# Layer 2's values and gates as seven half products, and weights split by two loads

## The chip, the cores and the metric

The kernel runs on one core of a Trainium2 chip. The metric is the device time of one execution in microseconds (us). Five engines work side by side, each through a queue of its own in order: TensorE (PE, products into PSUM; PEld is its load of the stationary operand), VectorE (DVE), ScalarE (ACT), GpSimd (POOL) and SyncE (SP, which here only issues DMAs). They wait for each other by semaphores. PSUM has eight banks of 128 x 512 f32.

## The reference

A trunk of two layers over 512 tokens of 2048 features, each layer normalizes its input, mixes, and adds to it. Layer 1 is a convolution branch and an attention branch; the change leaves it alone but for the end. Layer 2, which it touches, is a gated linear recurrence of 16 heads with a state of 128 x 128:

```python
h = rmsnorm(x, od_norm_g[j])
p = h @ od_w_in[j]                       # 2048 -> 4 x 2048
q, f_raw, i_val, g = _split(p, [HGRN_FDIM, HGRN_FDIM, D_MODEL, D_MODEL])
o = hgrn2(q, f_raw, i_val, lb_all[l], hgrn_norm_g[j]) * jax.nn.silu(g)
x = x + o @ od_w_out[j]
```

`i_val` are the values, `g` the gates. All is float32, and the output is normalized once more.

## The kernel before

**Precision.** TensorE works in float32r. Each operand is kept as two parts that add up to it: a rounded copy (ScalarE, `split_plain` or `split_scaled`) and the rest (VectorE). `mm3` makes three matmuls of one product: high by high, high by low, low by high.

**Weights.** They come in the order of use as 288 tiles of 512 KB, each two quarters [128, 512]. `prefetch` loads a tile on SP's queue into one of three buffers, `prepare` splits a quarter into one of four pairs `wh`, `wl`, two quarters ahead of use. A quarter feeds 12 matmuls (`quarter`).

**Chains.** Small dependent work (norms, attention, convolution, recurrence) is written as generators. `tick()` after each quarter moves every chain a step on, so that its instructions stand between dense matmuls; `finish` runs chains to their end with nothing between. TensorE's order is the order of the program; the other engines' is made by a scheduler.

**End of layer 1.** The output projection adds to `xa` (x, one [128, 512] tile per 128 features). In its last 16 columns `to_h1` makes the split, scaled `h1[c]` (names `hh`, `hl`) and sums squares into `acc1`. The factor 1/rms of layer 2 is made in a chain (`rstd_chain`) and applied to results: `rb1` along tokens as columns, `r1` for tokens as rows.

**Layer 2.** For each group of four heads, `value_rows` makes the values of four heads with tokens as rows: `h1` stationary, weights moving, 16 quarters of 12 matmuls into four banks. Then `head(h)` makes three dense products of four quarters each: query, decay (after which the recurrence `hgrn` of the head starts as a chain of 14 steps) and gate. From group 1 on, the projection of the four heads before (`w_out("ow", ...)`, 16 quarters) comes between values and heads. The steps of `hgrn` that the prediction speaks of: two radix stages (L680, with VectorE's L651 to L686), turning the keys (L741, L743), state sums (L747 to L751), output (L757, L759), its norm (squares L762, L764, power L765 on GpSimd, scaling L769), turning back and the gate (L773, L775).

Of the kernel before, what the change touches and what calls it, by code (L numbers as in the profile page):

```python
# [7 lines left out]
F32 = mybir.dt.float32  # L8
# [7 lines left out]
P = 128  # L16
# [12 lines left out]
N_WTILES = 288  # L29
LAST = 2 * N_WTILES - NK  # L30

# columns of the packed per-feature vectors
# [15 lines left out]
def trunk(ctx: ExitStack, tc: tile.TileContext, x, w, vec, cst, rope, msk, out, order):  # L48
# [6 lines left out]
    rawp = ctx.enter_context(tc.tile_pool(name="rawp", bufs=3))  # L55
    wsp = ctx.enter_context(tc.tile_pool(name="wsp", bufs=4))
# [18 lines left out]
    # chains of dependent steps, advanced by one step after each quarter of weights  # L75
# [19 lines left out]
    # the activation table and the tensor engine's clock come up while the first loads are under way  # L95
# [10 lines left out]
    # weights: a stream of quarters [128, 512], split into two float32r parts that add up exactly  # L106
    raws = []
    count = [0, 0]

    def prefetch(parts=1):  # L110
        raw = rawp.tile([P, 2 * S], F32, name="raw", tag="raw")
# [10 lines left out]
    def prepare():  # L122
# [5 lines left out]
        if n >= LAST:  # L128
            t = htile(n - LAST)
        else:  # L130
            t = (wsp.tile([P, S], F32R, name="wh", tag="wh"), wsp.tile([P, S], F32R, name="wl", tag="wl"))
        split_plain(src, *t)
        ready.append(t)

    def next_quarter(key):
# [3 lines left out]
        while len(ready) <= min(n + (AHEAD if n >= 16 else 0), 2 * N_WTILES - 1):  # L139
            prepare()  # L140
        return ready[n]
# [24 lines left out]
    def split_scaled(src, g, hi, lo):  # L166
        """hi + lo = src * g"""
# [47 lines left out]
    def silu2(src, rb, dst):  # L215
        """dst = 2 silu(src * rb)"""
# [7 lines left out]
    # ---------------------------------------------------------------- layer 0  # L224
# [55 lines left out]
    # lb = sigmoid(l1 - l0); la = (1 - lb) / 2  # L280
# [17 lines left out]
    # keep where query (partition) - key (free) >= 0  # L298
# [38 lines left out]
    # the high part on the lower half of the partitions, the low part on the upper one  # L337
# [167 lines left out]
    for g in range(2):  # L505
        # rotary part of the queries: x1 and x2 of four heads, 32 partitions each
# [17 lines left out]
        for j in range(4):  # L524
# [7 lines left out]
            # both parts of the rotary queries, each on both halves of the partitions  # L532
# [10 lines left out]
            # convolution groups spread over the heads  # L543
# [5 lines left out]
    # under the last head  # L549
# [4 lines left out]
    xp = ctx.enter_context(tc.tile_pool(name="xp", bufs=1, side="right", reuse_waits="tile"))  # L554
    xall = xp.tile([P, NK, S], F32, name="xall")
    xa = [xall[:, k, :] for k in range(NK)]

    def load_xa():
        for k in range(NK):
            nc.sync.dma_start(xa[k], x[:, k, :])  # L560
# [3 lines left out]
    spawn(load_xa())  # L564
# [6 lines left out]
    def w_out(name, rows, cols, after=None):  # L571
        n = len(rows)
        ops = [mix[r] for r in rows]
# [8 lines left out]

    acc1 = cp.tile([P, S], F32, name="acc", tag="acc")
    rb1 = cp.tile([P, S], F32, name="rb1", tag="rb")
    r1 = cp.tile([P, 4], F32, name="r1", tag="r0")
    h1 = []
    with ectx as cctx:
# [30 lines left out]
        def to_h1(c):  # L618
            h = htile(c)
            split_scaled(xa[c], vs[:, V_ODG + c:V_ODG + c + 1], *h)  # L620
            add_square(xa[c], acc1, c, pool)
            h1.append(h)

# [3 lines left out]
    # ---------------------------------------------------------------- layer 1  # L627
# [3 lines left out]
    c1 = spawn(rstd_chain(acc1, D, r1, rb1, 2))  # L631
# [331 lines left out]
```

## Time and profile before

| | us |
|---|---|
| median of three runs | 1790.07 (1789.45 to 1792.38) |
| span of the profiled execution, first to last instruction | 1787.5 |
| TensorE busy | 1768.7 (99%) |
| VectorE, ScalarE, GpSimd busy | 1150.6, 673.6, 83.1 |

The profiled execution's time is given as its span; what lies around the span is read from the difference to the runs, 2.6 us to the median. Busy TensorE means that some matmul is in it: matmuls overlap, so how fast it goes is read from their starts. An engine's idle time costs only where TensorE waits for it.

### The profile page before, as it was taken

How to read it: one execution, taken by the hardware profiler on the slowest of the kernel's cores; microseconds unless marked ns; L12 is line 12 of the kernel's file. 1: busy time of each engine (PE TensorE's matmuls, PEld its weight loads, DVE VectorE, ACT ScalarE, POOL GpSimd, SP SyncE). 2: the span in 40 equal slices, each digit the busy share in tenths (PEclk: the TensorE clock that was granted, in tenths of full speed). 3: DMA queues.
4: the chain of work that ended last, by engine and by line, in shares of the span. 5: the costliest groups of instructions: out<-in, count | busy, mean ns of one | idle time of the engine just before them, and what ended most of it. 6: DMA issues, size and time to landing. Idle time of an engine off the chain costs nothing.

```text
span 1787.5 us, 22387 instructions
## 1 busy us (share of the span) xinstructions
PE 1768.7 (99%) x8419; PEld 1470.5 (82%) x8419; DVE 1150.6 (64%) x2313; ACT 673.6 (38%) x1385; POOL 83.1 (5%) x86
## 2 busy tenths in 40 slices
PE   8999999999999999999999999999999999999997
PEld 6888888888888888888888888888888888888887
DVE  8554958595799775652677445776346774567766
ACT  6334444444443223452333222333323332333354
POOL 6000000000000000130000000000000000000000
PEclk9999999999999999999999999999999999999998
DMA  6222222222362232222222222222222222222232
GB/s 233 92 94 89 84 91 82 97 88 94 131 201 101 94 102 93 95 94 95 86 80 83 83 94 86 92 83 77 89 94 88 78 83 83 87 90 83 76 101 95
DMA packets 53612, 172.68 MB, mean 97 GB/s; under 512 B 5632, under 2 KB 9984, under 8 KB 53120
## 3 DMA queue, kind: packets, MB, share of 16 engines
q1 hardware_dynamic: 52928, 170.28, 28.2%
q8 instruction: 66, 1.08, 0.3%
q10 hardware_dynamic: 576, 0.97, 0.2%
q14 instruction: 42, 0.34, 0.1%
HBM read 163.89 MB, written 7.34 MB: 96 GB/s over the span
## 4 chain that ended last, share of the span: by engine, by line
PE 95%; DVE 2%; issue 2%; DMA 1%; ACT 0%; POOL 0%; POOLq 0%; DVEq 0%; ACTq 0%
PE mm L145 28%; PE mm L147 28%; PE mm L146 28%; PE aux L680 2%; PE aux L378 1%; PE aux L727 1%; PE aux L757 1%; DVE wl L173 1%; PE aux L759 1%; PE aux L747 1%; DVE hl L169 1%; DMA raw<-w 1%; PE aux L373 0%; PE aux L773 0%; PE aux L145 0%
## 5 line engine op out<-in xcount | busy, mean ns | idle before, releaser
L172 ACT ACTIVATE wh<-raw 128x512 fp32r<-128x512 f32 x560 | 352.2, 631 | 870.5 <-PE mm L146 737.6
L173 DVE TENSOR_TENSOR wl<-raw,wh 128x512 fp32r<-128x512 f32 x560 | 390.5, 699 | 356.8 <-ACT wh L172 342.2
L145 PE MATMUL mm<-hh,wh 128*128 128x512 f32 x1424 | 569.5, 400 | 1.4 <-ACT wh L172 1.4
L147 PE MATMUL mm<-hh,wl 128*128 128x512 f32 x1424 | 556.0, 390 | 3.0 <-DVE wl L173 3.0
L146 PE MATMUL mm<-hl,wh 128*128 128x512 f32 x1424 | 555.0, 390 | 0.7 <-DVE hl L169 0.7
L147 PEld LDWEIGHTS mm<-hh,wl 128*128 128x128 f32 x1424 | 267.3, 188 | 61.2 <-DVE wl L173 4.2
L145 PEld LDWEIGHTS mm<-hh,wh 128*128 128x128 f32 x1424 | 267.9, 188 | 54.5 <-ACT wh L172 2.3
L146 PEld LDWEIGHTS mm<-hl,wh 128*128 128x128 f32 x1424 | 267.8, 188 | 54.3 <-DVE hl L169 1.5
L427 DVE SCALAR_TENSOR_TENSOR y<-u,cwh,y 128x512 f32<-128x512 f32 x240 | 178.0, 745 | 2.5
L145 PE MATMUL mm<-mh,wh 128*128 128x512 f32 x448 | 178.1, 397 | 0.0
L147 PE MATMUL mm<-mh,wl 128*128 128x512 f32 x448 | 177.1, 395 | 0.0
L146 PE MATMUL mm<-ml,wh 128*128 128x512 f32 x448 | 177.0, 395 | 0.0
L579 DVE TENSOR_TENSOR xall<-xall,mm 128x512 f32<-128x512 f32 x96 | 65.8, 686 | 90.3 <-PE mm L147 90.3
L145 PE MATMUL mm<-wh,hh 128*128 128x512 f32 x256 | 102.1, 399 | 0.0
L147 PEld LDWEIGHTS mm<-mh,wl 128*128 128x128 f32 x448 | 84.2, 188 | 20.2
L146 PEld LDWEIGHTS mm<-ml,wh 128*128 128x128 f32 x448 | 84.2, 188 | 20.0
L145 PEld LDWEIGHTS mm<-mh,wh 128*128 128x128 f32 x448 | 84.2, 188 | 19.7
L147 PE MATMUL mm<-wh,hl 128*128 128x512 f32 x256 | 99.8, 390 | 0.0
L146 PE MATMUL mm<-wl,hh 128*128 128x512 f32 x256 | 99.7, 389 | 0.0
L147 PEld LDWEIGHTS mm<-wh,hl 128*128 128x128 f32 x256 | 48.0, 188 | 10.3
L146 PEld LDWEIGHTS mm<-wl,hh 128*128 128x128 f32 x256 | 48.1, 188 | 9.3
L145 PEld LDWEIGHTS mm<-wh,hh 128*128 128x128 f32 x256 | 48.1, 188 | 9.2
(229 smaller groups left out, 1906.1 us busy)
## 6 DMA issues: line engine op xcount, KB each, us to landing
raw<-w SPq DMA_DIRECT2D x287, 512.0 KB, 3.2
xall<-xT SPq DMA_DIRECT2D x16, 256.0 KB, 5.0
x<-xT SPq DMA_DIRECT2D x3, 1024.0 KB, 7.6
mix<-m SPq DMA_DIRECT2D x12, 256.0 KB, 2.0
m<-mix SPq DMA_DIRECT2D x12, 256.0 KB, 2.8
out<-xall SPq DMA_DIRECT2D x6, 512.0 KB, 3.1
x<-xT SPq DMA_DIRECT2D x4, 256.0 KB, 4.9
out<-xall SPq DMA_DIRECT2D x4, 256.0 KB, 3.5
```

The source lines that it names most:

```text
L145: pe.matmul(ps, a[0][:, asl], b[0][:, bsl], start=first, stop=False)
L146: pe.matmul(ps, a[0][:, asl], b[1][:, bsl], start=False, stop=False)
L147: pe.matmul(ps, a[1][:, asl], b[0][:, bsl], start=False, stop=last)
L169: dve.scalar_tensor_tensor(out=lo, in0=src, scalar=g, in1=hi.bitcast(F32), op0=ALU.mult, op1=ALU.subtract)
L172: act.activation(hi, src, AF.Copy)
L173: dve.tensor_tensor(out=lo, in0=src, in1=hi.bitcast(F32), op=ALU.subtract)
L378: pe.matmul(po[:, jb * P:], vr[:, jb, blocks(j)], pts[jb], start=jb == 0, stop=jb == 3)
L427: dve.scalar_tensor_tensor(out=y, in0=u[:, j:j + S], scalar=cwh[:, w0 + j:w0 + j + 1], in1=y, op0=ALU.mult, op1=ALU.add)
L579: dve.tensor_tensor(out=xa[c], in0=xa[c], in1=ps, op=ALU.add)
L680: pe.matmul(ps[:, i * 192:(i + 1) * 192], ks[:, blocks(g)], rhs, start=True, stop=True)
L727: pe.matmul(ps[:, blocks(g)], kb[:, blocks(g)], qb[:, blocks(g)], start=True, stop=True)
L747: pe.matmul(su[:, blocks(g)], kst[:, blocks(g)], vr[:, g, :], start=True, stop=True)
```

## The change

**Seven products.** Values and gates are cut in four sets of 1024 output columns (`SETS`). A set is a product of [512 tokens x 2048] with [2048 x 1024]; tokens, features and columns are halved, and the 2 x 2 blocks are multiplied by the Winograd form: seven products of half blocks and sums of blocks on both sides, and of results. A product has 4 items of 12 matmuls, 28 a set. The sums of `h1`'s blocks (S1 to S4) are made once, under the first set's first eight items, by `x_sums` from a copy `xd` of `xa` in DRAM; S1 stands in the place of the second half of `h1[0..7]`, which `restore` brings back in the last set. Sums of weight blocks (T1 to T4) are made per set on VectorE, T4 by an adding load. All four sets come ahead of the first head. Their results go to DRAM (`vd`, `gd`), and each head loads its gate, every fourth head its four heads' values.

**Weights after tile 128.** They are items: `Formed` ones loaded on SP's queue, summed where needed and split by ScalarE and VectorE; `Loaded` ones (the first eight, and all dense weights of layer 2 but the last eight tiles) loaded by GpSimd's queue into a float32r tile, copied negated by ScalarE, and loaded a second time, added, into the low part. `begin(n)` splits item n + 2 and starts loading item n + 3.

**Layer 2's loop.** `head` has two dense products. The projection of heads 0 to 3 (4 to 7) lies as columns between those of heads 5 to 7 (9 to 11). The rms factor goes into the head's norm, the gate ahead of turning back.

The diff, cut to its core:

```diff
+    class Loaded:
+        def first(self):
+            self.hi = hi_slot()
+            pool.dma_start(self.hi, self.src)
+        def second(self):
+            self.lo = lo_slot()
+            act.activation(self.lo, self.hi.bitcast(F32), AF.Copy, scale=-1.0)
+            pool.dma_start(self.lo, self.src, accum_op=ALU.add)
...
+    class Formed(Loaded):
+        def first(self):
+            self.raw = self.load()
+        def second(self):
+            src = self.form(self.raw)
+            self.hi, self.lo = hi_slot(), lo_slot()
+            split_plain(src, self.hi, self.lo)
...
+    def begin(n):
+        step_second(n + 2)
+        step_first(n + 3)
+        return items[n]
...
+    def x_sums(k):
+        t = ring("xr")
+        u = t.rearrange("p (a c) -> p a c", a=2)
+        for a in range(2):
+            nc.sync.dma_start(u[:, a, :], xd[:, k + 8 * a, :])
+            act.activation(u[:, a, :], u[:, a, :], AF.Copy, scale=vs[:, V_ODG + k + 8 * a:V_ODG + k + 8 * a + 1])
...
+        dve.tensor_tensor(out=s1, in0=a21, in1=a22, op=ALU.add)
+        dve.tensor_tensor(out=s2, in0=s1, in1=a11, op=ALU.subtract)
+        dve.tensor_tensor(out=s3, in0=a11, in1=a21, op=ALU.subtract)
+        dve.tensor_tensor(out=s4, in0=a12, in1=s2, op=ALU.subtract)
+        split_plain(s1, h1[k][0][:, H:], h1[k][1][:, H:])
+        split_plain(q[:, H:], *sums[k])
...
+    def product(ps, name, m):
+        it = begin(pos[0])
+        pos[0] += 1
+        for j in range(2):
+            k = 2 * m + j
+            a = operand(name, k)
+            for b in range(2):
+                mm3(ps[b], a, it.part(j), blocks(b), FULL, k == 0, k == 7)
+        tick()
...
+    for s_ in range(4):
+        p1, p2 = banks(), banks()
+        for m in range(4):
+            product(p1, "A11", m)
+            if s_ == 0:
+                x_sums(2 * m)
+                t1_raw(0, m)
+            product(p2, "A12", m)
+            if s_ == 0:
+                x_sums(2 * m + 1)
+                t1_sum(0, m)
...
+        for b in range(2):
+            result(s_, 0, b, p2[b], v[b])
+        p5, p6 = banks(), banks()
+        for m in range(4):
+            product(p5, "S1", m)
+            product(p6, "S2", m)
...
         rs = sm.tile([P, 4], F32, name="rs4", tag="rs4")
         dve.tensor_scalar(rs, ss, 1.0 / P, EPS, op0=ALU.mult, op1=ALU.add)
         pool.tensor_tensor(out=rs, in0=rs, in1=nhalf, op=ALU.pow)
+        pool.tensor_tensor(out=rs, in0=rs, in1=r1, op=ALU.mult)
         yield
         on = hgt("on")
         for g in range(4):
             act.activation(on[:, blocks(g)], po[:, blocks(g)], AF.Copy, scale=rs[:, g:g + 1])
+        dve.tensor_tensor(out=on, in0=on, in1=gate, op=ALU.mult)
...
-    for g in range(4):
-        value_rows(g)
-        if g in (1, 2):
-            finish(*heads)
-            w_out("ow", list(range(4 * g - 4, 4 * g)), range(NK))
-        for h in range(4 * g, 4 * g + 4):
-            head(h)
+    for h in range(16):
+        g, j = divmod(h, 4)
+        rows = list(range(4 * g - 4, 4 * g))
+        fill = [(rows, range(0))] * 2
+        if g in (1, 2) and j:
+            finish(*heads[:4 * g])
+            c = [0, 3, 5, 8, 10, 13, 16]
+            fill = [(rows, range(c[2 * j - 2 + i], c[2 * j - 1 + i])) for i in range(2)]
+        head(h, fill)
```

Where it moves instructions, first TensorE at the end of head 3's recurrence, before: matmuls of the next group's value rows (`mm<-wh,hh`, `mm<-wh,hl`, `mm<-wl,hh`) around the turning back of head 3 (`aux<-cs,on`).

```order
L145 MATMUL mm<-wh,hh_6663 128x512
L146 MATMUL mm<-wl,hh_6663 128x512
L147 MATMUL mm<-wh,hl_6664 128x512
L773 MATMUL aux<-cs,on 128x128 x4
L145 MATMUL mm<-wh,hh_6690 128x512
L146 MATMUL mm<-wl,hh_6690 128x512
```

And in the change, where head 5 begins: the last matmul of head 4's decay product, then all that is left of head 3, then head 5's query product.

```order
L223 MATMUL mm<-hh_6579,wl 128x512
L988 MATMUL aux<-X,ks 128x192 x4
L1052 MATMUL aux<-cs,ks 128x128 x3
L1058 MATMUL aux<-vr,kst 128x128 x3
L1068 MATMUL aux<-vr,at 128x128 x2
L1070 MATMUL aux<-st,X 128x128
L1068 MATMUL aux<-vr,at 128x128
L1070 MATMUL aux<-st,X 128x128
L1068 MATMUL aux<-vr,at 128x128
L1070 MATMUL aux<-st,X 128x128
L1087 MATMUL aux<-cs,on 128x128 x4
L221 MATMUL mm<-hh_6188,wh 128x512
```

The steps that stood a quarter apart now follow each other with no dense matmul between them.

Second, VectorE at the start of layer 2, before: the last columns of layer 1, the norm's factor, and 17 splits of the values' weights.

```order
L579 TENSOR_TENSOR xall<-xall,mm 128x512
L173 TENSOR_TENSOR wl<-raw,wh 128x512
L169 SCALAR_TENSOR_TENSOR hl_6820<-xall,vs,hh_6819 128x512
L173 TENSOR_TENSOR wl<-raw,wh 128x512 x2
L195 TENSOR_SCALAR rm<-aux 128x4
L203 TENSOR_SCALAR c<-cs,r_4279 128x128 x4
L173 TENSOR_TENSOR wl<-raw,wh 128x512 x17
```

And in the change, at the seam of the first set's first and second phase: the first result (`z<-mm,v`, which needs TensorE's eighth item), sums of activations (`xs`), their splits (`hl`, `fl`), a sum of weights (`ts<-rw`) and a split of one (`wl<-ts,wh`).

```order
L875 TENSOR_TENSOR z<-mm,v 128x512
L249 TENSOR_TENSOR fl_6610<-xs,fh_6609 128x768
L835 TENSOR_TENSOR xs<-xr 128x256
L875 TENSOR_TENSOR gate<-mm,v 128x512
L833 TENSOR_TENSOR xs<-xr 128x256
L249 TENSOR_TENSOR wl<-ts,wh 128x1024
L834 TENSOR_TENSOR xs<-xs,xr 128x256
L249 TENSOR_TENSOR hl_6291<-xs,hh_6290 128x256
L836 TENSOR_TENSOR xs<-xr,xs 128x256
L705 TENSOR_TENSOR ts<-rw 128x1024
L833 TENSOR_TENSOR xs<-xr 128x256
L249 TENSOR_TENSOR fl_6612<-xs,fh_6611 128x768
```

The next twelve rows go on in this way and hold the forming of T2 and its split:

```order
L834 TENSOR_TENSOR xs<-xs,xr 128x256
L835 TENSOR_TENSOR xs<-xr 128x256
L836 TENSOR_TENSOR xs<-xr,xs 128x256
L249 TENSOR_TENSOR hl_6316<-xs,hh_6315 128x256
L249 TENSOR_TENSOR fl_6614<-xs,fh_6613 128x768
L835 TENSOR_TENSOR xs<-xr 128x256
L833 TENSOR_TENSOR xs<-xr 128x256
L834 TENSOR_TENSOR xs<-xs,xr 128x256
L715 TENSOR_TENSOR ts<-rw,ts 128x1024
L836 TENSOR_TENSOR xs<-xr,xs 128x256
L249 TENSOR_TENSOR hl_6343<-xs,hh_6342 128x256
L249 TENSOR_TENSOR wl<-ts,wh 128x1024
```

Sums of activations that nothing needed before stand on VectorE between the weights' splits.

## Rows read from the trace of the kernel before

**Rows 1.** The page, first part: busy us, share of span, instructions.

```profile
PE 1768.7 (99%) x8419; PEld 1470.5 (82%) x8419; DVE 1150.6 (64%) x2313; ACT 673.6 (38%) x1385; POOL 83.1 (5%) x86
```

**Rows 2.** What TensorE waited for: us in total, times, longest.

```profile
PE mm L147 <- DVE wl L173: 3.0, 2, 2.5
```

**Rows 3.** Busy by stretch: us, engines' busy (instructions), granted clock, DMA share, GB/s.

```profile
785.00:831.50 46.50, 46.50 (x214) 38.73 (x213) 14.13 (x24) 14.21 (x24) 4.33 (x5) 1.00 0.27 91
870.72:910.05 39.33, 39.33 (x197) 33.43 (x196) 27.90 (x71) 14.00 (x36) 1.34 (x2) 1.00 0.26 85
...
1775.00:1780.00 5.00, 1.16 (x9) 0.91 (x8) 3.00 (x11) 0.14 (x1) 0.69 (x1) 0.83 0.00 1
```

**Rows 4.** TensorE in order of time: start, duration in us, line.

```profile
739.99 0.40 PE L145 MATMUL mm<-mh,wh 128*128 128x512 f32 x1
...
757.25 0.40 PE L147 MATMUL mm<-mh,wl 128*128 128x512 f32 x1
...
831.57 0.39 PE L145 MATMUL mm<-hh,wh 128*128 128x512 f32 x1
...
851.97 0.39 PE L145 MATMUL mm<-hh,wh 128*128 128x512 f32 x1
```

**Rows 5.** TensorE's groups in layer 2: count, busy us, mean ns, idle before.

```profile
L145 PE MATMUL mm<-hh,wh 128*128 128x512 f32 x768 | 307.9, 401 | 0.0
...
L145 PE MATMUL mm<-wh,hh 128*128 128x512 f32 x256 | 102.1, 399 | 0.0
```

**Rows 6.** VectorE's groups by shape, whole run.

```profile
L173 DVE TENSOR_TENSOR wl<-raw,wh 128x512 fp32r<-128x512 f32 x560 | 390.5, 699 | 356.8 <-ACT wh L172 342.2 <-PE aux L438 9.6 <-PE aux L378 3.9
...
L579 DVE TENSOR_TENSOR xall<-xall,mm 128x512 f32<-128x512 f32 x96 | 65.8, 686 | 90.3 <-PE mm L147 90.3
...
L169 DVE SCALAR_TENSOR_TENSOR hl<-x,vs,hh 128x512 fp32r<-128x512 f32 x16 | 19.7, 1264 | 0.6 <-ACT hh L168 0.6
...
L169 DVE SCALAR_TENSOR_TENSOR hl<-xall,vs,hh 128x512 fp32r<-128x512 f32 x16 | 12.0, 751 | 2.9 <-ACT hh L168 2.9
...
L715 DVE TENSOR_TENSOR qb<-q,pi 128x256 f32<-128x256 f32 x16 | 6.8, 422 | 0.0
```

**Rows 7.** ScalarE's groups by shape, whole run.

```profile
L172 ACT ACTIVATE wh<-raw 128x512 fp32r<-128x512 f32 x560 | 352.2, 631 | 870.5 <-PE mm L146 737.6 <-PE mm L147 123.7 <-issue 3.4
...
L180 ACT ACTIVATE c<-xall 128x256 f32<-128x256 f32 x28 | 11.7, 417 | 13.4 <-DVE xall L847 12.3 <-PE aux L206 1.1
...
L180 ACT ACTIVATE c<-xall 128x512 f32<-128x512 f32 x15 | 9.2, 615 | 0.0
```

**Rows 8.** One head's later steps in order of time.

```profile
916.65 1.46 PE L680 MATMUL aux<-X,ks 128*128 128x192 f32 x8
...
919.25 0.55 DVE L684 TENSOR_TENSOR X<-X,ab 128x384 f32<-128x384 f32 x1
919.72 0.55 DVE L686 TENSOR_TENSOR ks<-ks,ab 128x384 f32<-128x384 f32 x1
...
926.49 0.83 PE L747 MATMUL aux<-vr,kst 128*128 128x128 f32 x6
...
927.73 0.72 DVE L751 SCALAR_TENSOR_TENSOR st<-st,ab,aux 128x128 f32<-128x128 f32 x2
```

**Rows 9.** The last head's output and norm in order of time.

```profile
1702.56 0.39 PE L759 MATMUL aux<-st,X 128*128 128x128 f32 x2
...
1704.47 1.01 POOL L765 TENSOR_TENSOR rs<-rs,nhalf 128x4 f32<-128x4 f32 x1 [38.35 <-DVE rs L764]
...
1705.51 1.14 ACT L769 ACTIVATE on<-aux,rs 128x128 f32<-128x128 f32 x4 [1.32 <-POOL rs L765]
```

**Rows 10.** DMA queues (packets, MB, share) and issues (KB, us to landing).

```profile
q1 hardware_dynamic: 52928, 170.28, 28.2%
...
raw<-w SPq DMA_DIRECT2D x287, 512.0 KB, 3.2
...
x<-xT SPq DMA_DIRECT2D x3, 1024.0 KB, 7.6
```

More of the change, by code (lines that the diff above doesn't have):

```diff
@@ L47, in trunk @@
 @with_exitstack
-def trunk(ctx: ExitStack, tc: tile.TileContext, x, w, vec, cst, rope, msk, out, order):
+def trunk(ctx: ExitStack, tc: tile.TileContext, x, w, ws, vec, cst, rope, msk, out, order):
     nc = tc.nc
@@ L138, in next_quarter @@
         count[0] = n + 1
-        while len(ready) <= min(n + (AHEAD if n >= 16 else 0), 2 * N_WTILES - 1):
-            prepare()
-        return ready[n]
+        if n < 2 * N_EARLY:
+            while len(ready) <= min(n + (AHEAD if n >= 16 else 0), 2 * N_EARLY - 1):
+                prepare()
+            return ready[n]
+        if n % 2 == 0:
+            begin(pos[0])
+            pos[0] += 1
+        return items[pos[0] - 1].part(n % 2)
     def mm3(ps, a, b, asl, bsl, first, last):
@@ L572, in w_out @@
         n = len(rows)
+        if not len(cols):
+            return
         ops = [mix[r] for r in rows]
@@ L586, in trunk, with ring, __init__, first @@
     h1 = []
+    ph = [None]
+    nring = [0]
+    def ring(name):
+        nring[0] += 1
+        return ph[0].tile([P, 2 * S], F32, name=name, tag=f"r{nring[0] % 5}")
+    tsum = {}
+    class Formed(Loaded):
+        def __init__(self, load, form, after=None):
+            self.load, self.form, self.after = load, form, after
+        def first(self):
+            self.raw = self.load()
+        def second(self):
+            src = self.form(self.raw)
+            self.hi, self.lo = hi_slot(), lo_slot()
+            split_plain(src, self.hi, self.lo)
+            if self.after is not None:
+                self.after(self.raw)
@@ L587, in trunk, with restore @@
+    for i in range(N_EARLY, N_WTILES):
+        items.append(Loaded(w[i]) if 2 * i < LAST else Kept(w[i], 2 * i - LAST))
+    def restore():
+        for i in range(2):
+            t = ring("xr")
+            u = t.rearrange("p (a c) -> p a c", a=4)
+            nc.sync.dma_start(u, xd[:, 4 * i:4 * i + 4, H:])
+            for j in range(4):
+                k = 4 * i + j
+                split_scaled(u[:, j, :], vs[:, V_ODG + k:V_ODG + k + 1], h1[k][0][:, H:], h1[k][1][:, H:])
     with ectx as cctx:
@@ L624, in trunk @@
+            if c == 15:
+                step_first(3)
         finish(spawn(split_rows(range(4, 8))))
         w_out("ew", [4, 5, 6, 7], range(NK), to_h1)
+    xctx.close()
+    sctx = ExitStack()
+    fp = sctx.enter_context(tc.tile_pool(name="fp", bufs=1, reuse_waits="tile"))
+    ph[0] = sctx.enter_context(tc.tile_pool(name="ph", bufs=1, reuse_waits="tile"))
+    tpc[:] = [fp, "c"]
+    c1 = spawn(rstd_chain(acc1, D, r1, rb1, 2))
+    sums = [(fp.tile([P, 3 * H], F32R, name=f"fh{k}", tag=f"fh{k}"), fp.tile([P, 3 * H], F32R, name=f"fl{k}", tag=f"fl{k}"))
+            for k in range(8)]
@@ new lines, in operand, with banks @@
+    def operand(name, k):
+        if name in ("A11", "S1"):
+            return [t[:, (name == "S1") * H:][:, :H] for t in h1[k]]
+        if name in ("A12", "A22"):
+            return [t[:, (name == "A22") * H:][:, :H] for t in h1[k + 8]]
+        i = int(name[1]) - 2
+        return [t[:, i * H:(i + 1) * H] for t in sums[k]]
+    nbank = [0]
+    def banks():
+        r = []
+        for _ in range(2):
+            r.append(ps_mm() if nbank[0] % 8 < 5 else ps_x())
+            nbank[0] += 1
+        return r
@@ new lines, in product, with result @@
+    def product(ps, name, m):
+        it = begin(pos[0])
+        pos[0] += 1
+        for j in range(2):
+            k = 2 * m + j
[3 more added lines that the diff above has]
+        tick()
+    rh = fp.tile([P, 4], F32, name="rh")
+    vd = [dr.tile([P, 4, S], F32, name=f"vd{g}") for g in range(4)]
+    gd = [dr.tile([P, 4, S], F32, name=f"gd{g}") for g in range(4)]
+    def result(s_, col, b, in0, in1):
+        name, a = SETS[s_]
+        o = tp.tile([P, S], F32, name="z", tag="z") if b % 2 == 0 else tp.tile([P, S], F32, name="gate", tag="gate", bufs=2)
+        dve.tensor_tensor(out=o, in0=in0, in1=in1, op=ALU.add)
+        if name == "oi":
+            act.activation(o, o, AF.Copy, scale=r1[:, b:b + 1])
+        else:
+            t = tmp("th", bufs=1)
+            act.activation(t, o, AF.Tanh, scale=rh[:, b:b + 1])
+            dve.scalar_tensor_tensor(out=o, in0=t, scalar=1.0, in1=o, op0=ALU.add, op1=ALU.mult)
+        nc.sync.dma_start((vd if name == "oi" else gd)[2 * a + col][:, b, :], o)
```

207 lines of the change are left out of this document (164 added, 43 removed).

## The prediction

> **What bounds the kernel now.** I read the page's first part, then what TensorE waited for, then busy time by stretch, then TensorE's starts in order of time. TensorE is busy for 1768.7 of 1787.5 us [rows 1], and its longest wait on anybody sums to 3.0 us in two pieces [rows 2]. In the first value rows of layer 2 and in a head's period it is busy for the whole stretch at a granted clock of 1.00, its upper level of 2.4 GHz, while VectorE is at 27.90 of 39.33 us and ScalarE at 14.00 [rows 3]. So a matmul taken away shortens the time by one start-to-start step, and everything else costs only when TensorE has to wait for it. That step is read from starts, not from the 390 to 401 ns durations, which overlap: from 831.57 to 851.97 us there are 90 steps, 20.40 / 90 = 0.2267 us; under the output projection 739.99 to 757.25 is 74 steps, 0.2332 us [rows 4].
>
> **What goes.** Values and gates are 256 and 256 of the products per part: 3 x 256 with the weights moving, and a third of the 768 per part with the activations moving [rows 5], 1536 matmuls. Seven half products for each of four sets are 4 x 7 x 4 x 12 = 1344. TensorE's program falls from 7682 to 7490 rows, exactly those 192, so the saving is there as such: 192 x 0.2267 = **-43.5 us**. Were the new products at the slower step, 1344 x 0.0065 = 9 us of it would be lost; the nearest rows (weights moving, same kind of stretch) have the fast one, which I take. VectorE's copies of the gate (a product and a sum per head) only move.
>
> **What TensorE newly waits for: two ends of a recurrence.** Before, head 3 and head 7 were finished inside the next four heads' value rows: a step every 2.7 us, always with 12 matmuls between. Now `finish(*heads[:4 * g])` stands before head 5 and head 9, after 8 steps of head 3 and 11 of head 7 (three of its steps fall on output columns). The order shows what is left as one run without a dense matmul in it. Nothing queued behind it on TensorE may pass, so the next head's products wait. The idle part is read from a head of before. From the first radix product (916.65) to the keys ready (919.72 + 0.55) is 3.62 us, of which TensorE works 1.46: 2.2 idle; turning the keys and copying them adds about 0.5; from the state product (926.49) to the last state (927.73 + 0.72) is 1.96, some 0.45 of it work: 1.5 idle [rows 8]. From the end of the output product (1702.56 + 0.39) to the scaled rows (1705.51 + 1.14) it is 3.7 [rows 9], to which come a second GpSimd product (at most the 1.01 of the first [rows 9]; I take 0.9) and the gate product (0.69, as L579 [rows 6], and a handoff): 5.35. Head 3: 2.2 + 0.5 + 1.5 + 5.35 = 9.6; head 7 has only the last two parts: 6.9. Sum **+16.5 us**, between 12 (handoffs shorter, GpSimd's product short) and 22 (the granted clock falls in such a gap, as at the end of the run, where it was 0.83 in a stretch with 1.16 us of work in 5 [rows 3]).
>
> **The first set.** Each of its 28 items lasts 12 x 0.2267 = 2.72 us, half of a dense item. VectorE's queue decides. Two-input work of 512 and 256 columns takes 686 and 422 ns [rows 6], 1.03 ns a column, so 1024 columns are 1.21 us and 768 are 0.95; back to back each starts some 0.08 earlier (a row of 0.55 us that starts 0.47 after its like [rows 8]). VectorE waits for TensorE's eighth item at the first result (`z<-mm,v`), and from it to the split of the second item of the next phase (`ts<-rw,ts`, then `wl<-ts,wh`) are 24 instructions: 2 results of 512 columns, 15 of 256, 3 of 768, 4 of 1024; 15.4 us by durations, 13.5 with the overlap. TensorE has one item ready for that time: 13.5 - 2.7 = 11 us. Then one more sum set, a difference and a split for the fourth item of the phase: some 4 us. ScalarE has nearly as much in that stretch (copies of 512 at 0.63, 512 at 0.62 and 256 at 0.42 [rows 7], so about 1.0 for 1024): about 14 us, alongside. Before that the first set's loaded items have a lookahead of three, 8.2 us, for two transfers and a copy: a plain one lands in 3.2 [rows 10], 3.2 + 1.0 + 3.2 = 7.4, and GpSimd issues the second behind the next item's first. I put 3 there. Sum **+18 us**, between 8 (only the loaded items and half of VectorE's run) and 34 (transfers of the sums, 4.2 MB, the blocks, 4.2 MB, and the loaded items beside each other: at 85 GB/s for a share of 0.26 [rows 3], so 1.6 us for 512 KB, they fill some 45 us of queue in a phase of 22).
>
> **The other sets and the seams.** A set is 76.1 us on TensorE. VectorE has 28 splits and 12 sums at 1.21 and 14 results at 0.69: 58, with gates 5.5 more: 76 to 84%, so it is covered except at the seams; +3 (0 to 20). The first dense item comes behind half-length ones and its second transfer about 1.5 us late: +1.5 (0 to 5). The head's own VectorE work falls: 27.9 less 12 splits at 0.70 and the gate, in 39.33 - 48 x 0.2267 = 28.5 us; no wait there is taken.
>
> **The loads that split.** 88 items now go through GpSimd's queue twice each: a load that rounds, ScalarE's negated copy, and a load that adds. Before, that queue issued no DMA at all: all 170 MB went by q1 [rows 10]. No row has such a load, so it is bounded: below by a plain one, 1.6 us of all queues, landing in 3.2; above by 1024 KB beside others, 7.6 us to landing [rows 10], 3.8 per 512 KB. At either end a head's four items need 4 x (1.6 + 1.6) or 4 x (1.6 + 3.8) plus 1.6 for gate and values: 14 to 23 of 28.5 us. I take zero, nearer the plain row. VectorE loses 0.70 per split [rows 6], which nobody waited for. On price, the Trainium skill's page "Collectives: The Full Stack" (section "The bandwidth ceiling: the fold count and why AG ≠ RS ≠ AR") says that an add in a transfer reads two sources, about twice the traffic; by it the adding load would be 3.2 us and the term stays zero. No run so far shows it.
>
> GpSimd and VectorE do disturb each other: the same VectorE instruction took 1264 ns in layer 0, beside GpSimd's sums, and 751 later [rows 6]. The Trainium skill, "SBUF — State Buffer", section "Who interferes with whom", speaks against the change here: one-input VectorE work in its two-port mode keeps GpSimd from writing, and descriptors of its loads are such writes, while two-input work only meets GpSimd's reads. By it only the heads' `f` (0.43 us each) would hold an issue, 7 us at most; by the row alone any VectorE work might, which is the slower rival.
>
> **Sum.** -43.5 + 16.5 + 18 + 3 + 1.5 = -4.5 us. Span 1787.5 - 4.5 = 1783.0; the median of the three runs, 1790.07, is 2.6 above the profiled span, so **1785 us** in a run. Own range 1775 to 1796.
>
> **Rivals.** (a) GpSimd's queue becomes the bound of the heads and output columns: 16 x 28.5 + 48 x 2.8 = 590 us of TensorE against 88 x (1.6 + a) + 16 x 1.6 + 12.8 for the reloaded x. They are equal at a = 4.7 us for an adding load, and each 0.1 above costs 9 us. At 5.3 it is 1785 + 55 = 1840. For it: no such load in the trace, the 1264 ns; against: queues at a share of 0.26 and plain loads at 1.6. (b) The waits are half as long, because VectorE's run in the first set hides under TensorE's wait for loaded weights and GpSimd's second product is short: 8 + 12 + 1 in place of 39, 1785 - 18 = 1767. For it: GpSimd's 1.01 us is a power, the new one a product; against: the order puts VectorE's wait for the eighth item ahead of the run. (c) VectorE, at 84% and with bursts of results, makes TensorE wait at every phase: 7 us more for each of three sets, 1806. For it: lookahead is 8.2 us and a gate burst 6.8; against: before, with 0.70 per 2.7 us, it never did.
>
> **Chances.** Forecast 0.45, (a) 0.20, (b) 0.22, (c) 0.13. A measurement here tells 0.2% from no change, 1786.5 to 1793.7: half of the forecast's case lies below it, a third inside. Faster 0.22 + 0.22 = 0.44; same 0.18; slower 0.20 + 0.13 and a tenth of the forecast's case, 0.38. Range 1760 to 1840: part of (b) below and of (a) above are left out.
>
> **What would show it.** Right: two TensorE gaps of 7 to 10 us ahead of dense matmuls after head transposes; 10 to 15 us before the tenth item of the first set, released by VectorE's `wl<-ts`; head periods of 28.5 us. Wrong: dense matmuls waiting for loads on GpSimd's queue (a), head gaps of a few us each, or products at 0.233 us.

## The result, and the profile after

The changed kernel takes 1832.76 us (median of three runs, 1832.11 to 1834.38) against 1790.07, a ratio of 1.0235 with a 95% interval of [1.0217, 1.0253]. It is slower; the forecast was 1785, a little faster. The profiled span went from 1787.5 to 1830.2, up 42.7 us. First the page of the changed kernel: busy time, then in 40 slices the granted clock and the share of the DMA queues, then the two queues, SP's (hardware) and GpSimd's (software).

```profile
PE 1753.9 (96%) x8227; PEld 1451.7 (79%) x8227; DVE 1193.8 (65%) x2258; ACT 734.6 (40%) x1345; POOL 239.2 (13%) x310
...
PEclk9999999999999999987999999999899999999998
DMA  6222222222552232498676775977577867877752
...
q0 software_dynamic: 29952, 109.07, 28.1%
q1 hardware_dynamic: 65888, 169.24, 27.3%
```

TensorE was busy for 99% [rows 1] and is for 96%. In the slices where layer 2 begins the granted clock falls while the queues' share goes from 2 to 9 tenths. What TensorE waited for (us in total, times, longest), against the 3.0 us in two pieces of before [rows 2]:

```profile
PE aux L221 <- ACT wh L248: 13.6, 2, 11.6
PE mm L222 <- DMA wl<-ws: 12.9, 4, 7.0
PE aux L1087 <- DVE on L1083: 10.9, 4, 5.5
PE mm L223 <- DMA wl<-w: 6.4, 2, 5.7
PE aux L222 <- DVE wl L249: 3.8, 2, 3.3
PE aux L1087 <- DVE ab L979: 3.2, 1, 3.2
```

Rows 1, 2 and 5 are the first set (`ws` are its weights), row 4 the first weights of the heads (`w`), rows 3 and 6 the recurrence's turning back. The first set by stretches of 10 us, in the columns of [rows 3]: length, busy PE, PEld, DVE, ACT and POOL with instructions, granted clock, DMA share, GB/s.

```profile
805.00:815.00 10.00, 7.46 (x22) 5.92 (x23) 3.69 (x10) 2.82 (x4) 1.44 (x2) 0.60 1.05 316
815.00:825.00 10.00, 5.68 (x21) 4.49 (x20) 4.46 (x8) 5.90 (x10) 1.73 (x2) 0.74 1.03 254
825.00:835.00 10.00, 9.76 (x39) 7.44 (x37) 7.47 (x13) 7.89 (x13) 0.00 (x0) 0.92 0.71 211
835.00:845.00 10.00, 0.00 (x0) 0.00 (x0) 8.36 (x16) 5.91 (x9) 0.00 (x0) 0.60 0.80 274
845.00:855.00 10.00, 7.71 (x24) 5.57 (x24) 9.19 (x14) 5.91 (x8) 0.86 (x1) 0.72 0.70 190
855.00:865.00 10.00, 5.07 (x13) 3.86 (x14) 5.03 (x5) 4.71 (x5) 1.72 (x2) 0.66 0.96 324
```

Read the last two columns beside the busy times of VectorE and ScalarE: from 805 to 825 the queues are full, VectorE is not half busy, and ScalarE is busy for 28% and 59%. Only in the hole from 835 and in the 10 us behind it is VectorE near full (8.36 and 9.19 of 10). The forecast's figure for this stretch came from VectorE. And a wait costs more than its length. TensorE's matmuls behind the 7.00 us wait (start, duration, engine, line):

```profile
807.54 0.79 PE L222 MATMUL mm<-wl,hh 128*128 128x512 f32 x1 [7.00 <-DMA wl<-ws]
808.14 0.63 PE L223 MATMUL mm<-wh,hl 128*128 128x512 f32 x1
808.56 0.63 PE L221 MATMUL mm<-wh,hh 128*128 128x512 f32 x1
...
812.40 0.63 PE L221 MATMUL mm<-wh,hh 128*128 128x512 f32 x1
...
813.86 0.39 PE L223 MATMUL mm<-wh,hl 128*128 128x512 f32 x1
```

From 807.54 to 812.83 there are 12 steps of 0.44 us in place of 0.2267, 2.6 us more: the granted clock is at its lower level of 1.2 GHz (0.50 in the rows of 5 us there) after the wait, and back at 2.4 by 813.

Four stretches measure the terms, and the experiments are compared by them. From the first set's first product (788.88) to its 289th (898.03), where its last phase begins: 109.15 us, of which 288 x 0.2267 = 65.3 is the products' own and 1.6 the norm's matmuls, which before had too; 42.3 are lost. From there to the last set's last phase (1131.22): 233.19 for 1008 products, 228.5 of their own, 4.7 lost. From the first dense product of head 0 (1142.10) to its recurrence's first product (1187.34) there are 156 matmuls, 35.37 us of their own in 45.24: 9.9 lost. The heads' stretch, from 1142.10 to the first matmul of the last projection, is 625.84 us.

What stood where the prediction expected a gap: the end of head 3's recurrence (idle before, and releaser), then that of head 7.

```profile
1286.45 0.52 PE L1052 MATMUL aux<-cs,ks 128*128 128x128 f32 x3 [1.94 <-DVE ks L994]
1287.55 1.65 PE L1058 MATMUL aux<-vr,kst 128*128 128x128 f32 x6 [0.58 <-ACT kst L1054]
1292.55 0.49 PE L1070 MATMUL aux<-st,X 128*128 128x128 f32 x2 [1.05 <-DVE st L1062]
1298.11 1.09 PE L1087 MATMUL aux<-cs,on 128*128 128x128 f32 x4 [5.07 <-DVE on L1083]
...
1464.33 1.09 PE L1087 MATMUL aux<-cs,on 128*128 128x128 f32 x4 [5.45 <-DVE on L1083]
```

### The profile page after: what moved, and what is told of

It is laid out like the page before. It is cut to its first block, busy times and chain, and to the rows that moved or that the text cites. A ratio compares the mean times of both kernels' runs of the same rounds, so it can differ in the third digit from the quotient of the medians.

```text
span 1830.2 us, 22277 instructions
## 1 busy us (share of the span) xinstructions
PE 1753.9 (96%) x8227; PEld 1451.7 (79%) x8227; DVE 1193.8 (65%) x2258; ACT 734.6 (40%) x1345; POOL 239.2 (13%) x310
## 3 DMA queue, kind: packets, MB, share of 16 engines
q0 software_dynamic: 29952, 109.07, 28.1%
## 4 chain that ended last, share of the span: by engine, by line
PE 83%; DVE 6%; DMA 5%; issue 3%; ACT 2%; POOL 1%; POOLq 0%; DVEq 0%; ACTq 0%; SPq 0%
PE mm L223 23%; PE mm L222 23%; PE mm L221 23%; PE aux L988 2%; PE aux L222 2%; PE aux L221 2%; PE aux L223 2%; DMA rw<-ws 2%; PE aux L454 1%; DVE wl L249 1%; PE aux L1035 1%; DVE hl L245 1%; DMA wh<-w 1%; DMA wl<-w 1%; DVE wq L249 1%
## 5 line engine op out<-in xcount | busy, mean ns | idle before, releaser
L221 PE MATMUL mm<-hh,wq 128*128 128x512 f32 x656 | 263.0, 401 | 2.3 <-ACT wq L248 2.3
L249 DVE TENSOR_TENSOR wq<-raw,wq 128x512 fp32r<-128x512 f32 x256 | 183.7, 720 | 120.1 <-ACT wq L248 119.5
L223 PE MATMUL mm<-hh,wq 128*128 128x512 f32 x656 | 257.4, 392 | 2.8 <-DVE wq L249 2.8
L222 PE MATMUL mm<-hl,wq 128*128 128x512 f32 x656 | 256.8, 391 | 0.0
L221 PE MATMUL mm<-hh,wh 128*128 128x512 f32 x512 | 210.1, 410 | 0.0
L223 PE MATMUL mm<-hh,wl 128*128 128x512 f32 x512 | 203.3, 397 | 6.4 <-DMA wl<-w 6.4
L222 PE MATMUL mm<-hl,wh 128*128 128x512 f32 x512 | 202.7, 396 | 0.0
L223 PEld LDWEIGHTS mm<-hh,wq 128*128 128x128 f32 x656 | 123.8, 189 | 30.4 <-DVE wq L249 3.9
L221 PEld LDWEIGHTS mm<-hh,wq 128*128 128x128 f32 x656 | 124.3, 190 | 27.9 <-ACT wq L248 2.8
L222 PEld LDWEIGHTS mm<-hl,wh 128*128 128x128 f32 x512 | 98.4, 192 | 18.8
L221 PEld LDWEIGHTS mm<-hh,wh 128*128 128x128 f32 x512 | 98.5, 192 | 18.5
L221 PE MATMUL mm<-mh,wq 128*128 128x512 f32 x256 | 101.6, 397 | 0.0
L223 PE MATMUL mm<-mh,wq 128*128 128x512 f32 x256 | 101.2, 395 | 0.0
```

The lines of the kernel that those rows point to most:

```text
L221: pe.matmul(ps, a[0][:, asl], b[0][:, bsl], start=first, stop=False)
L222: pe.matmul(ps, a[0][:, asl], b[1][:, bsl], start=False, stop=False)
L223: pe.matmul(ps, a[1][:, asl], b[0][:, bsl], start=False, stop=last)
L249: dve.tensor_tensor(out=lo, in0=src, in1=hi.bitcast(F32), op=ALU.subtract)
```

## The experiments

Theory B is the prediction's: in the first set VectorE's queue decides. Theory A: the transfers do, since blocks, sums and twice-loaded weights must come within 22 us. Theory C came up on the way: five shared buffers (`ring`), which SP's queue waits for in order.

**late_columns.** The projection starts a head later.

```diff
-        if g in (1, 2) and j:
+        if g in (1, 2) and j > 1:
             finish(*heads[:4 * g])
-            c = [0, 3, 5, 8, 10, 13, 16]
+            c = [0, 4, 8, 12, 16]
```

> The projection of heads 0 to 3 (4 to 7) starts at head 6 (10) in place of head 5 (9), so head 3 (7) has 16 ticks, more than its 14 steps, before its rows are needed. Theory (the two ends of a recurrence cost what the changed kernel's trace shows there: 11 us of waits and 1.5 of slower matmuls at 1286 to 1299, 5.5 and 0.8 at 1464): both waits gone, TensorE's span 17 to 20 us shorter, 1813 to 1816 us in a run; the third wait of that kind (3.2 us at 1636, no end of a recurrence) stays. Rival (the chains only get late elsewhere: heads 4 and 5 now run denser against the columns, the same VectorE and ScalarE work, or the tiles for seven heads' results come free later): waits of the same sum ahead of the columns of head 6 and 10, 1828 to 1833 us.

Measured: 1809.22 us, 23.5 less; the heads' stretch is 601.39, 24.45 less. Of waits on VectorE there, this is left:

```profile
PE aux L1087 <- DVE on L1083: 1.5, 2, 0.7
```

Both ends are gone, and so is the third wait, which was expected to stay: the gain is above the 17 to 20 us expected. In the changed kernel VectorE reached that head's norm (`rs<-ss`, L1075) at 1631.25, behind two reciprocals of 1.7 us of the next head's start; here it reaches it at 1609.48, ahead of the reciprocals at 1611.32 and 1613.53. The third wait cost 3.15 us and 2.5 more in the 12 slower steps behind it, so of the 24.45 some 19 belong to the two ends.

**sums_from_sbuf, sums_no_adds, no_adding_loads.** Each takes one suspect from the first set.

```diff
-            nc.sync.dma_start(u[:, a, :], xd[:, k + 8 * a, :])
-            act.activation(u[:, a, :], u[:, a, :], AF.Copy, scale=...)
+            act.activation(u[:, a, :], h1[k + 8][0].bitcast(F32), AF.Copy, scale=...)
```

```diff
-        q = ring("xs")
-        s1, s2, s3, s4 = [q[:, i * H:(i + 1) * H] for i in range(4)]
-        dve.tensor_tensor(out=s1, in0=a21, in1=a22, op=ALU.add)
-        dve.tensor_tensor(out=s2, in0=s1, in1=a11, op=ALU.subtract)
-        dve.tensor_tensor(out=s3, in0=a11, in1=a21, op=ALU.subtract)
-        dve.tensor_tensor(out=s4, in0=a12, in1=s2, op=ALU.subtract)
+        q = t
+        s1 = t[:, :H]
+        ring("xs")
```

```diff
             act.activation(self.lo, self.hi.bitcast(F32), AF.Copy, scale=-1.0)
-            pool.dma_start(self.lo, self.src, accum_op=ALU.add)
```

> x_sums reads the high parts of h1[8..15] from SBUF in place of the 16 loads of 256 KB from xd (the numbers are then not those of the reference); ScalarE's and VectorE's instructions are the same in number and shape. Theory A (the first set waits for transfers, the queues are at 1.0 of their time there): 4.2 MB of some 20 MB less and no landing of 5 us inside each sum; TensorE's first set up to its last product, 109.2 us in the changed kernel, falls by 15 to 25 us, a run takes 1808 to 1818 us. Theory B (VectorE's queue decides, as predicted): its work is the same, the stretch falls by 5 us at most, 1828 us or more.

> The four sums and differences of each x_sums are left out (the blocks themselves are split in their place, so the numbers are not those of the reference): 32 VectorE instructions of 256 columns fewer, 32 x 0.34 = 11 us of VectorE's time in the first set; the loads and ScalarE's work stay. Theory B (VectorE decides): the first set's 109.2 us fall by 9 to 13, 1820 to 1824 us. Theory A (transfers decide): under 4 us, 1829 to 1833 us.

> Every second, adding load of a weight tile is left out (the low part is then only the negated high part, not the reference's numbers), 96 transfers; ScalarE's copies and the first loads stay. Theory A (transfers): the waits of the first set's loaded items (12.9 us and some 6 of slower matmuls) and of the first head's weights (6.4 and some 2) vanish, 20 to 28 us, 1804 to 1812 us. Theory B (VectorE): the first set's wait moves to the items behind, only the first head's wait goes, 8 to 14 us, 1818 to 1824 us. In the heads: if GpSimd's queue or the adding loads bound them, their period of 28.0 to 28.7 us falls; if not, it stays within 0.2.

Measured: 1818.18, 1830.84 and 1806.77 us; the first set 96.45, 104.21 and 95.08 in place of 109.15. So 12.7 us for the loads of `xd`, 14.1 for the adding loads (whose absence also took 11.8 from the heads' stretch, 9.9 of it at the first head), and 4.9 for 11 us of VectorE's work, of which 1.9 reached the run. That is A's order, not B's, but not A's figures throughout: sums_from_sbuf took 12.7 off the set where A expected 15 to 25, and 1818.18 us where it expected 1818 at most; sums_no_adds took 4.9 off the set, between A's 4 and B's 9. The 1.9 of the run is not clear of noise (its four runs lie between 1828.51 and 1836.86), and its edit also leaves one of each sum's two shared buffers unused, so the 4.9 is not VectorE's work alone. Without adding loads the first phase ran nearly through, and one wait stood behind it, which gave rise to theory C. Its row, and the software queue there:

```profile
PE aux L220 <- ACT wh L247: 15.7, 1, 15.7
```

```profile
q0 software_dynamic: 16128, 58.73, 11.6%
```

Behind ScalarE's split stood VectorE's queue, as in the prediction: its instructions from the first result (815.38) to its own split of the tenth item (ending at 834.22) took 18.8 us, with some 3 of idle time in it, and ScalarE waited for one of them. So B's "wait moves to the items behind" held for this wait, though not for the time.

The queue's row prices the adding load: 28.1% of 1830.2 us less 11.6% of 1805.3 is 304.9 us of all queues for 96 loads, 3.18 each, against 1.6 for a plain one of 512 KB [rows 10]. The Trainium skill's rule that the prediction cited ("Collectives: The Full Stack", section "The bandwidth ceiling: the fold count and why AG ≠ RS ≠ AR": the add of a reduce step reads two sources) gave an estimate of 3.2; this trace agrees with the price, and no run here shows whether two reads make it. Heads without projection columns started 28.0 to 28.7 us apart with these loads and without, so they bound no head.

**fewer_transfers, fewer_transfers_no_adds.** The first and third edits together, then all three.

> Both the adding loads and the 16 loads of xd are left out (not the reference's numbers). Theory A (transfers alone decide the first set): the two parts add up, its 109.2 us fall by 12.7 + 14.1 = 27 to some 82, a run by 14.6 + 26.0 to 1790 to 1794 us, and what is left is ScalarE and VectorE in turn. Rival C (the five buffers of the sums are a second limit behind the transfers, whose wait of 15.7 us stood in the run without adding loads): a wait of 10 us or more for the first item of the second phase stays, 1796 to 1802 us.

> The adding loads, the loads of xd and the four sums and differences of each x_sums are left out (not the reference's numbers). In the changed kernel, leaving out the 32 sums gave 5 of the first set's 109.2 us; without the transfers VectorE was busy for 9.85 and 10.00 of 10 us from 805 to 825 and the first set took 82.4. Theory (two limits in a row: the transfers first, VectorE's queue behind them): the 11 us of VectorE's time now count, the set falls to 70 to 75 us and a run to 1784 to 1789. Rival (what is left is ScalarE, 10.00 and 9.66 of 10 in the same stretch): under 4 us, 1792 to 1796.

Measured: 1795.71 and 1795.11 us, the set 82.37 and 81.61. The two transfers' parts add up in the set (expected 82), though the run lies 1.7 above the 1790 to 1794 that A expected; the wait of 15.7 shrank to 4.4, so C in the form expected (10 or more) did not hold. With the transfers out of the way VectorE is full just where the prediction had put it (the rows from 805 of fewer_transfers):

```profile
805.00:815.00 10.00, 8.55 (x41) 7.08 (x41) 9.85 (x22) 10.00 (x17) 0.01 (x1) 1.00 0.67 208
815.00:825.00 10.00, 4.75 (x19) 3.25 (x17) 10.00 (x19) 9.66 (x15) 0.00 (x0) 0.86 0.59 183
```

Yet 11 us less of that work gave 0.8 of the set. In that run VectorE itself waited for a weight block, and TensorE for VectorE:

```profile
816.52 1.23 DVE L704 TENSOR_TENSOR ts<-rw 128x1024 f32<-128x1024 f32 x1 [4.23 <-DMA rw<-ws]
```

```profile
820.13 0.80 PE L221 MATMUL mm<-wl,hh 128*128 128x512 f32 x1 [4.47 <-DVE wl L248]
```

A full engine was again not the bound: the theory expected 7 to 12. The time is what the rival (ScalarE) expected, but behind that load ScalarE too waited, 2.66 us for VectorE's sum. What holds the last 15 us (81.6 less 65.3 and 1.6) is not settled: the block's load, ScalarE and VectorE follow each other.

**sums_in_place.** SP's queue in the changed kernel, from 786 to 862 us, waited mostly for VectorE to be done with a buffer:

```profile
SPq L710 <- DVE xs L836: 11.2, 4, 5.3
SPq L828 <- DVE xs L833: 7.4, 1, 7.4
SPq L710 <- DMA rw<-ws: 7.3, 2, 4.6
```

```diff
-        q = ring("xs")
-        s1, s2, s3, s4 = [q[:, i * H:(i + 1) * H] for i in range(4)]
+        s1, s2, s3, s4 = a22, a11, a21, a12
...
-        split_plain(q[:, H:], *sums[k])
+        split_plain(t[:, :3 * H], *sums[k])
```

> The changed kernel, the four sums of x_sums written over the four blocks that they are made of, so each takes one of the five shared buffers in place of two; loads, ScalarE and VectorE instructions stay the same in number and shape (VectorE's two middle ones change places), and so do the results. Theory C (in the first set SP's queue, in order, stands still because no buffer is free: of the stretch 786 to 862 it waited some 45 us for VectorE to be done with one): the first set's 109.2 us fall by 8 to 16, a run to 1816 to 1824 us. Theory A (only the amount that is moved counts): under 4 us, 1829 to 1833 us.

Measured: 1828.26 us, 4.5 less, the set 104.13, 5.0 less: between the two theories, and as much as sums_no_adds gave, here with VectorE's work unchanged. What TensorE waited for:

```profile
PE mm L222 <- DMA wl<-ws: 18.3, 7, 8.2
...
PE aux L222 <- DVE wl L249: 5.3, 4, 2.4
...
PE aux L221 <- ACT wh L248: 2.1, 1, 2.1
```

The two long waits for the split (13.6) are down to 2.1, and the waits for loads went from 12.9 to 18.3. With buffers free earlier the later waits shrink, but the first eight items take 48.95 us in place of 43.00: the waits for loads come forward. So the buffers hold something back, and behind them stand the transfers.

**plain_first_set.** The first set as eight products, so that the same sums have 65 us in place of 22.

```diff
+    for c in range(2):
+        ps = banks() + banks()
+        for n in range(8):
+            it = begin(pos[0])
+            pos[0] += 1
+            for j in range(2):
+                k = 2 * n + j
+                for b in range(4):
+                    mm3(ps[b], h1[k], it.part(j), blocks(b), FULL, k == 0, k == 15)
+            tick()
+            if 8 * c + n in (1, 2, 4, 5, 7, 8, 10, 11):
+                x_sums((1, 2, 4, 5, 7, 8, 10, 11).index(8 * c + n))
...
-    for s_ in range(4):
+    for s_ in range(1, 4):
```

> The first set as eight products (384 matmuls in place of 336, 12 of its 16 items loaded plainly on SP's queue), the sums of h1's blocks spread over 12 of these items of 5.4 us in place of 8 of 2.7. Theory (43.9 us are lost in the first set because its transfers and sums must come within 22 us, not because the sums are made at all): first set 87.1 us and 2 to 6 of waits, 42 lost us less and 48 x 0.2267 = 10.9 more, 1801 to 1808 us. Rival (the sums' chain of load, scale, sums and splits through five buffers takes 40 us or more of waits wherever it stands, or the next set's first items run into the same shortage): 1820 us or more.

Measured: 1806.25 us, 26.5 less, with 48 matmuls more. The first 288 of its products take 68.61 us, 3.3 above their own time, with 1.2 us of waits for a load. Made over 65 us, the sums cost 3.3 us at most. This run also has four items with an adding load in the set in place of eight, and forms no sums of this set's weights; how much each of the three gave, it does not show.

**late_reload, seam, held_reload.** The wait for the first head's weights.

```diff
     xall = open_xa(ctx)
-    spawn(load_xa(xd))
...
         head(h, fill)
+        if h == 0:
+            spawn(load_xa(xd))
```

```diff
-        items.append(Loaded(w[i]) if
+        items.append(Formed(lambda i=i: tile(i), lambda t: t) if i < N_EARLY + 2 else Loaded(w[i]) if
```

```diff
+            if held[0] is not None:
+                act.activation(xa[k][:, 0:4], held[0][:, 0:4], AF.Copy)
             nc.sync.dma_start(xa[k], src[:, k, :])
```

> The 16 loads that bring x back (4.2 MB) start after head 0 in place of ahead of it. Theory (they fill the queues while the first head's weights are loaded: queues at 1.0 of their time and an adding load landing in 8.5 us there, 6.0 over the whole run): the waits of 5.7 and 0.7 us at 1148 and 1163 fall to 2 together and the slower matmuls behind them go, 5 to 8 us, 1825 to 1828 us. Rival (the lookahead of three half-length items, 8.2 us, is too short for two loads and a copy anyway, and GpSimd's first load waits 30 us for its buffer until TensorE frees it): at least 4 us of wait stay, 1829 to 1833 us.

> The changed kernel with one edit: the first two weight tiles of the heads are loaded once on SP's queue into the sums' buffers and split by ScalarE and VectorE, in place of a rounding and an adding load that must wait for a buffer of their own. Theory (lookahead: behind items of 2.7 us the loads start 8.2 us before their use, and two loads and a copy take 13): the wait of 5.7 us at 1148 goes, and the slower matmuls behind it, 6 to 9 us, 1824 to 1827 us. Rival (the queues are full there, whatever is loaded): 3 us or less, 1830 to 1833 us.

> The reload of x is now held back by data: four columns of each tile are first written from the newest head's query, so that its load can't be issued before that head. Starting it later in the program alone moved nothing, since SP's queue ran ahead and issued it at 1136 as before. Theory (the 16 loads fill the queues while the first head's weights come): no reload before 1160, the waits of 5.7 and 0.7 us at 1148 and 1163 fall to 2 or less, 4 to 8 us, 1825 to 1829 us. Rival (lookahead of 8.2 us too short for two loads and a copy even with free queues, 4 + 1 + 4 at least): 3 us or more of the wait stay, 1829 to 1832 us.

late_reload took 1832.66 us and lost 9.9 us at the first head as before, but tells nothing: its reload still began at 1136.15 (1137.04 in the changed kernel), since nothing on SP's queue held it. held_reload keeps that edit and adds a dependency; its reload begins at 1160.99, it takes 1825.47 us, 7.3 less, and loses 7.0 at the first head, so that 2.9 of the 7.3 come from there (in its profile layer 2 also starts 1.4 us earlier). One wait of the two is left there, of the size that the rival expected:

```profile
PE mm L223 <- DMA wl<-w: 4.1, 1, 4.1
```

seam takes 1825.91 us, 6.9 less, loses 5.4 there, and its waits are 1.8 and 1.3 us. So both are at work, neither theory alone: with the reload away the lookahead still costs most of the 9.9, and with the lookahead mended 5.4 stay. With both edits, in combined_held below, the stretch loses 1.7, after 5.0 in combined_seams, which has no dependency on the reload. Without the adding loads at all, and with the reload, the stretch loses nothing (35.36 us in no_adding_loads). GpSimd's first load in the changed kernel, and its idle time ahead of it, say why the lookahead is short:

```profile
1134.40 0.55 POOL L162 DMA_DIRECT2D wh<-w  x1 [29.78 <-PE aux L223]
```

It can't be issued before TensorE frees the buffer, three items of 2.7 us ahead of use.

**combined, combined_seams, combined_held.** late_columns, late_reload and plain_first_set; then seam's edit with an earlier plain load of the fourth item and a later return of `h1`'s halves; then held_reload's edit.

> Late columns, late reload and the eight-product first set together. If the three act at different places, as their places in the trace say, 1832.8 - 23.5 - 27 - 6 = 1776 us (1770 to 1785), 0.3 to 1.1% below the kernel before. Rival (each takes the room that hid something for another): 1790 us or more.

> The combined kernel with the same edit, the fourth item of the first set loaded plainly, and the return of h1's halves begun two items later, in the last items of its phase. The combined kernel lost 5.7 and 1.6 us in steps of TensorE at the first heads' weights, 3.1 at the fourth item, 1.7 and 2.7 in the phase with the return, and some 4 in slower matmuls behind them. Theory (all four are lookahead): 12 to 16 us, 1765 to 1769 us. Rival (they come back at the next item): 1775 us or more.

> The same on the fastest kernel so far (1767.0 us), which still waited 2.5 us for a head's weights at 1123 with the reload beside it. Theory: that wait goes, 2 to 5 us, 1762 to 1765 us. Rival (the reload only meets other heads' loads later, or the query's tile is held longer): 1766 us or more.

Measured: 1781.09 us (0.9948 of before, [0.9936, 0.9961]), 1767.03 (0.9870, [0.9854, 0.9887]) and 1763.12 (0.9852, [0.9839, 0.9866]). The first came out 5 us above the 1776 expected, within its 1770 to 1785; the sum counted 6 for late_reload, which gave none. The other two came out as expected. The fastest, its page and TensorE's waits in layer 2 up to 1700 us:

```profile
PE 1738.9 (99%) x8275; PEld 1444.6 (82%) x8275; DVE 1166.6 (66%) x2227; ACT 719.5 (41%) x1343; POOL 226.3 (13%) x292
...
PEclk9999999999999999999999999999999999999998
```

```profile
PE aux L1113 <- DVE on L1109: 1.5, 2, 0.7
PE mm L223 <- DMA wl<-w: 1.4, 1, 1.4
```

Three sets of seven products keep 144 of the 192 matmuls saved, 32.6 us, and some 27 of it arrive. The busy shares of VectorE and ScalarE are those of the changed kernel to within a point: nearly the same work, with time around it.

## Why the prediction was wrong

| term, us | forecast | measured | from |
|---|---|---|---|
| 192 matmuls fewer | -43.5 | -43.5 | products 0.2267 apart |
| ends of the recurrence | +16.5 | +24.5, of it some 19 at the two ends | late_columns, heads' stretch |
| first set | +18 | +42.3 | 109.15 - 65.3 - 1.6 |
| of it: its first eight items | 3 | 19.6 | 43.00 - 21.8 - 1.6 |
| of it: its next four | 11 + 4 | 22.0 | 32.92 - 10.9 |
| other sets | +3 | +4.7 | 233.2 - 228.5 |
| first dense item | +1.5 | +9.9 | 45.24 - 35.37 |
| heads' adding loads | 0 | 0 | no_adding_loads, head periods |
| sum | -4.5 | +37.9 | |

The span grew by 42.7. Of the 4.8 that are missing 2.7 lie ahead of layer 2 (its first product starts at 788.88, before at 786.18; in the experiments, with the same layer 1, at 786.7 to 790.7), and 2.1 are not placed.

**The saving** was right, at the fast step: the rows of the later sets, as from 936.11 to 938.83, are 2.72 us for 12.

**The step that failed is "VectorE's queue decides", with 3 us for the loads ahead of it.** The first set's +18 was 3 for the loaded items, 11 for VectorE's 24 instructions behind the first result, and 4 for the fourth item of that phase. Those 24 came in the forecast order and took 16.1 us against 13.5, from 831.40 to 847.53:

```profile
831.40 0.69 DVE L875 TENSOR_TENSOR z<-mm,v 128x512 f32<-128x512 f32 x1 [0.47 <-PE mm L223]
...
843.95 1.23 DVE L715 TENSOR_TENSOR ts<-rw,ts 128x1024 f32<-128x1024 f32 x1 [0.59 <-DMA rw<-ws]
...
846.30 1.23 DVE L249 TENSOR_TENSOR wl<-ts,wh 128x1024 fp32r<-128x1024 f32 x1 [0.45 <-ACT wh L248]
```

TensorE's wait behind them, before the tenth item, was as long as forecast, released by ScalarE's split of the same tile:

```profile
846.32 0.79 PE L221 MATMUL aux<-wh,fh 128*128 128x512 f32 x1 [11.56 <-ACT wh L248]
```

What the sum lacked stands mostly ahead of this. The first eight items took 43.00 us, of which 21.8 are their own and 1.6 the norm's: 19.6 were lost, 12.9 in waits for loads and the rest in slower steps behind them, where the sum had 3. The queues were busy for 0.98 of that stretch, 42 us of transfers in a phase of 21.8:

```profile
788.88:831.88 43.00, 30.10 (x113) 23.35 (x112) 16.84 (x35) 19.65 (x29) 10.67 (x13) 0.80 0.98 276
```

The transfers were in the prediction too, as 45 us of queue in a phase of 22, but only as an upper bound of 34, and with 1.6 us for every 512 KB (by its own terms that makes 51; with adding loads at 3.18 it is 64, some of it outside the eight items). The runs take the parts of the loss away one at a time (us from first product to first product):

| | first eight items | next four | last twelve |
|---|---|---|---|
| the products' own time | 21.8 | 10.9 | 32.6 |
| the changed kernel | 43.0 | 32.9 | 33.2 |
| no_adding_loads | 27.8 | 33.6 | 33.7 |
| sums_from_sbuf | 44.6 | 16.3 | 35.5 |
| fewer_transfers | 26.3 | 20.7 | 35.4 |
| sums_no_adds | 50.2 | 13.1 | 41.0 |

The adding loads hold the first eight items. The loads of `xd` make VectorE's run behind the first result: the last four of the eight pairs were issued only at 827.91, 832.99, 837.53 and 845.20, and with the same VectorE instructions but without these loads, 7.9 us lie between the first result and that split. Without the 32 sums VectorE's run is gone too, but then the first eight items take 7 us longer, with the queues at 1.03, and a wait of 6.1 comes at the sixteenth item. So the wait that was to show the step right came, and the trace alone would have let the step pass; that 11 us less of VectorE's work gave 4.9 of the set, and 27 came with the transfers, shows that VectorE's queue was not what decided. One reservation: the scheduler orders VectorE's instructions anew for each of these kernels, so a run shows the effect of its edit with the order that follows from it.

**The two ends** were seen in place and kind. Their waits, 8.6 and 5.5 us against 9.6 and 6.9, were a little shorter than forecast; with the lower clock in and behind them they cost some 19, inside the 12 to 22. What made 24.5 of it is the third wait of 3.2 and the slower steps behind it, which the sum did not have.

**The first dense item**: the mechanism was named, the size was not. The first adding load landed in 8.5 us there, not in 3.2, beside a reload that the sum had left out of this place.

**Rivals.** (a) did not come: the heads go at TensorE's pace, and an adding load costs 3.18, below the 4.7 at which GpSimd's queue would have decided. (b) did not come, the waits were longer. (c), VectorE in every phase, was wrong in kind: the other sets lost 4.7 together. The case that came about, full queues in the first set, had no rival of its own; it was the upper bound of one term. That the range up to 1840 holds 1832.76 is luck: 1840 was (a)'s figure, and the forecast's own range ended at 1796.

## What to carry to other kernels

Where a change brings new loads into a short phase, sum the queues' time of that phase, twice-loaded tiles at their own price, before looking at any engine; a mean share of 0.26 before says nothing of it. When work is taken out of the bound engine, what used to hide under it must be given its time back, and giving a quarter of the saving away for that was the cheapest way tried here. A load that stands later in the program is not later for that (1136.15 us against 1137.04 here): what held it back was a dependency on data (1160.99).

## What the runs showed of the hardware

A load that adds into SBUF costs 3.18 us of all queues for 512 KB, twice a plain one (1.6), and lands in 6.0 us over the heads (`wl<-w`), a rounding one in 3.7:

```profile
wh<-w POOLq DMA_DIRECT2D x88, 512.0 KB, 3.7
wl<-w POOLq DMA_DIRECT2D x88, 512.0 KB, 6.0
```

Each of the six waits of 4 us or more in this kernel (4.3 to 11.6) was followed by matmuls at the lower clock, as were shorter ones (2.2 at 1116, 3.2 at 1636): in the first set the waits sum to 30.6 us, and some 12 of the 42.3 lost lie in slower steps behind them.
